# Splitting the first load into parts of every eighth partition, with one part loaded through GpSimd's queue

**Chip, cores, metric.** One core of one Trainium2 chip. Times are device microseconds (us) of one execution. A kernel's time is the median of its runs; the profile is of one of those runs, and its span is some 1.8 us shorter than the time.

## What the kernel computes

```python
x = abs(randn(32, 512, 1024)) + 1e-6          # float32, 67.1 MB
out = np.sum(1.0 / x, axis=-1)                # (32, 512) float32
```

The 16,384 rows of 1024 values lie as 128 partitions x 128 rows. For each of its rows a partition adds up the reciprocals; one half of a row is handled together with the other half, as (a + b) / (a * b), with the division done by logarithm and exponential.

Of the kernel before, what the change touches and what calls it, by code (L numbers as in the profile page):

```python
# [11 lines left out]
def kernel(  # L12
# [15 lines left out]
    nc = tc.nc  # L28
    f32 = mybir.dt.float32
    P = 128  # L30
    D = 1024
# [7 lines left out]


    A, B, C = (2, 0, 0), (2, 2, 0), (2, 2, 1)
    LOADS = [[A, B, A, B], [A, B, A, C]] * 5 + [[A, B], [A, C]] * 3



# [21 lines left out]
    x_v = x.flatten_outer_dims().rearrange("(p f) d -> p f d", p=P)  # L67
# [13 lines left out]
    opool = ctx.enter_context(tc.tile_pool(name="opool", bufs=1))  # L81
# [10 lines left out]
    ring = opool.tile([P, R, D], f32)  # L92
    sums = opool.tile([P, F], f32)
    ident = opool.tile([P, P], f32)
    make_identity(nc, ident)
    keep = tc.keep_in_program_order

    def add(bank, *halves):
        for k, half in enumerate(halves):
            i = nc.tensor.matmul(  # L100
                bank,
                lhsT=ident,
                rhs=half,
                start=k == 0,
                stop=k == len(halves) - 1,
            )
            keep(i)

    def sum_row(c, row, fac, out=None):
        i = nc.vector.tensor_tensor_reduce(  # L110
            out=row if out is None else out,
            in0=row,
            in1=fac,
            scale=S,
            scalar=0.0,
            op0=mult,
            op1=plus,
            accum_out=sums[:, c : c + 1],
        )
        keep(i)  # L120

    def sum_rows(c, xc, pr, sm, rc):
        m, e = xc.shape[1], len(sm)
        for j in range(e, m):
            row = xc[:, j, :].rearrange("p (h e) -> p h e", h=2)
            sum_row(
                c + j,
                row,
                rc[j - e].unsqueeze(1).to_broadcast([P, 2, H]),
                pr[:, e : e + 2, :] if j == e and e + 1 < m else None,  # L130
            )
        for j in reversed(range(e)):
            sum_row(c + j, pr[:, j, :], sm[j])

    waiting = None
    c0 = 0
    for chunks in LOADS:
        n = sum(m for m, _, _ in chunks)
        xt = ring[:, c0 % R : c0 % R + n, :]
        keep(nc.sync.dma_start(out=xt, in_=x_v[:, c0 : c0 + n, :]))  # L140

        made, q = [], 0
        for m, e, v in chunks:
            pr = ppool.tile([P, m, H], f32, tag="ps" if e else "pr")
            for j in range(v):
                b = bpool.tile([P, H], f32, tag="b")
                add(b, xt[:, q + j, H:])
                i = nc.vector.tensor_tensor(  # L148
                    out=pr[:, j, :], in0=xt[:, q + j, :H], in1=b, op=mult
                )  # L150
                keep(i)
            made.append(pr)
            q += m

        q = 0
        for (m, e, v), pr in zip(chunks, made):
            xc = xt[:, q : q + m, :]
            if v < m:
                i = nc.gpsimd.tensor_tensor(  # L159
                    out=pr[:, v:, :], in0=xc[:, v:, :H], in1=xc[:, v:, H:], op=mult  # L160
                )
                keep(i)
            sm = []
            for j in range(e):
                s = spool.tile([P, H], f32, tag="s")
                add(s, xc[:, j, :H], xc[:, j, H:])
                sm.append(s)
            if waiting:
                sum_rows(*waiting)
            keep(nc.scalar.activation(out=pr, in_=pr, func=Ln, scale=S))  # L170
            rc = []
            if e < m:
                r = rpool.tile([P, m - e, H], f32, tag="rc")
                keep(
                    nc.scalar.activation(out=r, in_=pr[:, e:, :], func=Exp, scale=-1.0)  # L175
                )
                rc = [r[:, l, :] for l in range(m - e)]
            if e:
                r = pr[:, :e, :]
                keep(nc.scalar.activation(out=r, in_=r, func=Exp, scale=-1.0))  # L180
            waiting = c0 + q, xc, pr, sm, rc
            q += m
        c0 += n
    assert c0 == LAST, c0

    c0 = LAST
    for n in LAST_LOADS:
        xt = ring[:, c0 % R : c0 % R + n, :]
# [17 lines left out]
    for op in order:  # L206
        kind, c, n = op[0], int(op[1:].rstrip("+")), 1 + op.endswith("+")
        j = (c - LAST) % 2
        rows = ring[:, c % R : c % R + n, :]
# [10 lines left out]
        elif kind == "V":  # L220
            keep(
                nc.vector.tensor_tensor(  # L222
                    out=pr[:, 0, :], in0=a[:, 0, :], in1=bs[c], op=mult
# [18 lines left out]
        elif kind == "T":  # L242
            row = rows[:, 0, :].rearrange("p (h e) -> p h e", h=2)
            k = (c - LAST) // 2
# [5 lines left out]
        elif kind == "X":  # L250
            keep(
                nc.scalar.activation(
                    out=rows,
                    in_=rows,
# [37 lines left out]
```

## The kernel before

The parts that matter here are the loads. `ring` holds 40 rows for each partition; a load brings 8 or 4 rows (later 2 or 1) of all 128 partitions, so a load of 8 rows is 128 packets of 32 KB, one for each partition. Sixteen DMA engines carry the packets, as the profile counts them; the trace before records sixteen partial landings for each of the 30 loads, on eight completion semaphores in turn, and a load has landed with the last of its sixteen (load 1: last one at 13.55 us, first multiply at 13.62).

```python
A, B, C = (2, 0, 0), (2, 2, 0), (2, 2, 1)     # a chunk: rows, rows with sums by TensorE, rows multiplied by VectorE
LOADS = [[A, B, A, B], [A, B, A, C]] * 5 + [[A, B], [A, C]] * 3
...
x_v = x.flatten_outer_dims().rearrange("(p f) d -> p f d", p=P)
ring = opool.tile([P, R, D], f32)
...
c0 = 0
for chunks in LOADS:
    n = sum(m for m, _, _ in chunks)
    xt = ring[:, c0 % R : c0 % R + n, :]
    keep(nc.sync.dma_start(out=xt, in_=x_v[:, c0 : c0 + n, :]))
    ...   # per chunk: GpSimd multiplies the halves (A), or TensorE adds them as well (B, C)
          # ScalarE: logarithm, then exponential; VectorE: product and row sum
```

## Time and profile before

| | before |
|---|---|
| time, median (lowest to highest) | 169.75 us (169.62 to 170.16), of three runs |
| read from HBM | 67.11 MB, 400 GB/s over the span of 167.9 us |
| busy share: TensorE, VectorE, ScalarE, GpSimd | 78%, 73%, 80%, 82% |
| DMA engines' share | 94.4% |

No compute engine is busy as much as the sixteen DMA engines are. The views that carry the argument are in the prediction. For the comparison below, here is the rate of the DMA engines in the profile's 40 slices (each 4.2 us), then three stretches from the table of stretches of the kernel before. The columns of a stretch: start and end, length, busy time and number of instructions of TensorE, its weight loads, VectorE, ScalarE and GpSimd, the granted clock of TensorE, the DMA share and GB/s. A packet is counted whole in the stretch where it starts, so that a share can come out above 1.

```profile
GB/s 195 429 437 429 445 429 437 437 429 429 406 455 414 445 422 449 422 431 437 429 429 429 429 398 429 427 433 433 420 429 408 423 418 424 422 422 414 382 26 18
```

### The profile page before, as it was taken

The numbers are of one execution on the slowest core, as the hardware profiler recorded it, in microseconds if no ns is written. First come the engines' busy times: TensorE is split into PE (matmuls) and PEld (weight loads), VectorE is DVE, ScalarE is ACT, GpSimd is POOL, SyncE is SP. The second block draws the span as 40 slices with busy tenths as digits, with TensorE's granted clock in tenths as the row PEclk, the third lists the DMA queues.
The fourth block names the chain that finished last, engine by engine and source line by source line (L and its number), as shares of the span: only waits on it lengthen the run. The fifth ranks groups of instructions, "written<-read, shape, count | busy, mean of one in ns | idle before, by whom it ended". The sixth has DMA issues, their size and how long they took to land.

```text
span 167.9 us, 1307 instructions
## 1 busy us (share of the span) xinstructions
PE 130.8 (78%) x278; PEld 50.5 (30%) x278; DVE 122.8 (73%) x268; ACT 134.1 (80%) x143; POOL 137.7 (82%) x73
## 2 busy tenths in 40 slices
PE   0007999786989869776797869877999988799991
PEld 0003333232323323222332323333343324243340
DVE  0000677768977677885777787778989898999894
ACT  3001898979888897959879787999999998999992
POOL 1007999699996999859996998999999999979780
PEclk9999999999999999999999999999999999999999
DMA  6999999999999999999999999999999999999900
GB/s 195 429 437 429 445 429 437 437 429 429 406 455 414 445 422 449 422 431 437 429 429 429 429 398 429 427 433 433 420 429 408 423 418 424 422 422 414 382 26 18
DMA packets 4471, 67.25 MB, mean 401 GB/s; under 512 B 496, under 2 KB 624, under 8 KB 1136
## 3 DMA queue, kind: packets, MB, share of 16 engines
q1 hardware_dynamic: 4464, 67.18, 94.4%
q8 instruction: 2, 0.03, 0.1%
q14 instruction: 5, 0.04, 0.1%
HBM read 67.11 MB, written 0.07 MB: 400 GB/s over the span
## 4 chain that ended last, share of the span: by engine, by line
DMA 71%; ACT 11%; POOL 10%; DVE 3%; issue 2%; PE 2%; DVEq 0%; SPq 0%; POOLq 0%; ACTq 0%
DMA ring<-in_x_dram 71%; POOL pr L159 8%; ACT pr L231 5%; ACT pr L237 3%; ACT r L237 2%; POOL pr L213 1%; DVE pr L110 1%; PE s L100 1%; DVE ring L110 1%; ACT pr L170 1%; ACT r L175 1%; PE bb L100 1%; DVE pr L222 0%; DVE sums L110 0%; DVEq L287 0%
## 5 line engine op out<-in xcount | busy, mean ns | idle before, releaser
L100 PE MATMUL s<-ring,ident 128*128 128x512 f32 x256 | 121.4, 613 | 32.2 <-DMA ring<-in_x_dram 16.2
L159 POOL TENSOR_TENSOR pr<-ring 128x1024 f32<-128x1024 f32 (+1 forms) x52 | 112.7, 2202 | 21.5 <-DMA ring<-in_x_dram 21.5
L100 PEld LDWEIGHTS s<-ring,ident 128*128 128x128 f32 x256 | 46.9, 193 | 104.1 <-issue 63.3
L170 ACT ACTIVATE pr<-pr 128x1024 f32<-128x1024 f32 x52 | 54.8, 1053 | 26.9 <-POOL pr L159 26.9
L110 DVE CUSTOM_DVE_ANT_1 pr<-ring,r 128x1024 f32<-128x1024 f32 x27 | 33.0, 1221 | 41.4 <-ACT r L175 41.4
L110 DVE CUSTOM_DVE_ANT_1 ring<-ring,r 128x1024 f32<-128x1024 f32 x37 | 44.8, 1217 | 0.2 <-issue 0.2
L110 DVE CUSTOM_DVE_ANT_0 pr<-pr,s 128x512 f32<-128x512 f32 x64 | 41.5, 683 | 0.3 <-ACT pr L237 0.3
L180 ACT ACTIVATE pr<-pr 128x1024 f32<-128x1024 f32 x26 | 27.5, 1057 | 0.8
L175 ACT ACTIVATE r<-pr 128x1024 f32<-128x1024 f32 x26 | 26.7, 1028 | 0.8
L213 POOL TENSOR_TENSOR pr<-ring 128x512 f32<-128x512 f32 (+1 forms) x15 | 24.5, 1648 | 3.0 <-DMA ring<-in_x_dram 2.4
L231 ACT ACTIVATE pr<-pr 128x512 f32<-128x512 f32 (+1 forms) x17 | 13.0, 794 | 1.0 <-DVE pr L222 0.7
L110 DVE DVE_READ_ACCUMULATOR2_ANT sums<- 128x1 f32 x128 | 10.6, 83 | 0.0
L100 PE MATMUL b<-ring,ident 128*128 128x512 f32 x16 | 8.7, 625 | 0.1
L237 ACT ACTIVATE pr<-pr 128x512 f32<-128x512 f32 (+1 forms) x10 | 6.9, 704 | 0.1
L237 ACT ACTIVATE r<-pr 128x512 f32<-128x512 f32 (+1 forms) x11 | 6.8, 625 | 0.1
L148 DVE TENSOR_TENSOR pr<-ring,b 128x512 f32<-128x512 f32 x8 | 5.5, 682 | 0.0
L100 PEld LDWEIGHTS b<-ring,ident 128*128 128x128 f32 x16 | 2.6, 188 | 5.6 <-DMA ring<-in_x_dram 4.1
L100 PE MATMUL bb<-ring,ident 128*128 128x512 f32 x6 | 3.2, 622 | 1.3 <-DMA ring<-in_x_dram 1.2
L222 DVE TENSOR_TENSOR pr<-ring,bb 128x512 f32<-128x512 f32 x3 | 2.1, 686 | 0.7 <-PE bb L100 0.6
L100 PEld LDWEIGHTS bb<-ring,ident 128*128 128x128 f32 x6 | 1.0, 188 | 3.4 <-DVE sums L110 2.0
L71 ACT ACT_TABLE_LOAD x1 | 1.3, 1283 | 0.7 <-PEq L276 0.7
L215 DVE TENSOR_TENSOR pr<-ring 128x512 f32<-128x512 f32 x1 | 0.9, 864 | 0.0
(6 smaller groups left out, 0.9 us busy)
## 6 DMA issues: line engine op xcount, KB each, us to landing
ring<-in_x_dram SPq DMA_DIRECT2D x10, 4096.0 KB, 37.8
ring<-in_x_dram SPq DMA_DIRECT2D x6, 2048.0 KB, 37.0
ring<-in_x_dram SPq DMA_DIRECT2D x10, 1024.0 KB, 26.0
ring<-in_x_dram SPq DMA_DIRECT2D x4, 512.0 KB, 16.8
out_dram<-sums SPq DMA_DIRECT2D x1, 64.0 KB, 1.5
```

The lines of the kernel that those rows point to most:

```text
L71: nc.scalar.add_instruction(mybir.InstLoadActFuncSet(name=nc.get_next_instruction_name(), act_func_set_id=act_sets.index("natural_log_exp_ ...
L100: i = nc.tensor.matmul(bank, lhsT=ident, rhs=half, start=k == 0, stop=k == len(halves) - 1,)
L110: i = nc.vector.tensor_tensor_reduce(out=row if out is None else out, in0=row, in1=fac, scale=S, scalar=0.0, op0=mult, op1=plus, accum_out ...
L148: i = nc.vector.tensor_tensor(out=pr[:, j, :], in0=xt[:, q + j, :H], in1=b, op=mult)
L159: i = nc.gpsimd.tensor_tensor(out=pr[:, v:, :], in0=xc[:, v:, :H], in1=xc[:, v:, H:], op=mult)
L170: keep(nc.scalar.activation(out=pr, in_=pr, func=Ln, scale=S))
L175: nc.scalar.activation(out=r, in_=pr[:, e:, :], func=Exp, scale=-1.0)
L180: keep(nc.scalar.activation(out=r, in_=r, func=Exp, scale=-1.0))
L213: keep(nc.gpsimd.tensor_tensor(out=pr, in0=a, in1=b, op=mult))
L222: nc.vector.tensor_tensor(out=pr[:, 0, :], in0=a[:, 0, :], in1=bs[c], op=mult)
L231: keep(nc.scalar.activation(out=pr, in_=pr, func=Ln, scale=S))
L237: keep(nc.scalar.activation(out=r, in_=pr, func=Exp, scale=-1.0))
```

## The change

The intent, as far as the code tells it: some DMA engines end later than others (in the kernel before the last load landed at 159.38 to 160.21 us on thirteen and at 161.29 to 161.46 on three), and moving one 16 KB packet from each of eight engines to the other eight should even this out. To do so, one half of the first load (rows 0 to 3) is cut into eight parts of 16 partitions each. Seven go by SyncE; the eighth goes by GpSimd's queue as two transfers of eight partitions, each behind a load of one element a partition into `spare` ("one-element load" below) that is meant to steer it onto one half of the engines. (The prediction calls the halves lower and upper; the traces do not number the engines.) The other half (rows 4 to 7) is loaded first and whole.

```diff
-    LOADS = [[A, B, A, B], [A, B, A, C]] * 5 + [[A, B], [A, C]] * 3
+    LOADS = [[B, B, A, A], [A, B, A, C]] + [[A, B, A, B], [A, B, A, C]] * 4
+    LOADS += [[A, B], [A, C]] * 3
...
+    spare = opool.tile([P, 1, 1], f32)
...
+    def first_load(xt, n):
+        h = n // 2
+        for g in range(0, P, P // 2):
+            for dst, rows, w in ((spare, 1, 1), (xt, h, D)):
+                at = slice(g, g + P // 2, 8)
+                keep(nc.gpsimd.dma_start(out=dst[at, :rows, :w], in_=x_v[at, :rows, :w]))
+        keep(nc.sync.dma_start(out=xt[:, h:, :], in_=x_v[:, h:n, :]))
+        for k in range(1, 8):
+            at = slice(k, P, 8)
+            keep(nc.sync.dma_start(out=xt[at, :h, :], in_=x_v[at, :h, :]))
...
-        keep(nc.sync.dma_start(out=xt, in_=x_v[:, c0 : c0 + n, :]))
+        if c0 == 0:
+            first_load(xt, n)
+        else:
+            keep(nc.sync.dma_start(out=xt, in_=x_v[:, c0 : c0 + n, :]))
```

More of the change, by code (lines that the diff above doesn't have):

```diff
@@ L133, in sum_rows @@
             sum_row(c + j, pr[:, j, :], sm[j])
+    def first_load(xt, n):
[3 more added lines that the diff above has]
+                at = slice(g, g + P // 2, 8)
+                keep(
+                    nc.gpsimd.dma_start(
+                        out=dst[at, :rows, :w], in_=x_v[at, :rows, :w]
+                    )
+                )
+        keep(nc.sync.dma_start(out=xt[:, h:, :], in_=x_v[:, h:n, :]))
+        for k in range(1, 8):
+            at = slice(k, P, 8)
+            keep(nc.sync.dma_start(out=xt[at, :h, :], in_=x_v[at, :h, :]))
     waiting = None
```

## The prediction

> **What bounds the kernel now.** I read the page first (slices, DMA rows, chain), then the table of stretches, the waits, the waits of the DMA-issuing queue, and the timeline of the first 14 us and of the tail.
>
> ```profile
> DMA  6999999999999999999999999999999999999900
> q1 hardware_dynamic: 4464, 67.18, 94.4%
> q8 instruction: 2, 0.03, 0.1%
> q14 instruction: 5, 0.04, 0.1%
> DMA 71%; ACT 11%; POOL 10%; DVE 3%; issue 2%; PE 2%; DVEq 0%; SPq 0%; POOLq 0%; ACTq 0%
> ```
>
> The DMA engines are full from slice 2 to slice 38, and the chain that ended last is 71% transfers. Two more queues, q8 and q14, carry seven small packets of instructions: whatever engine carries one of those loses time that the other fifteen do not lose.
>
> ```profile
> 1.70:13.60 11.90, 0.00 (x0) 0.00 (x0) 0.00 (x0) 0.32 (x1) 0.00 (x0) 1.00 1.02 413
> 60.00:100.00 40.00, 32.05 (x68) 12.01 (x68) 30.33 (x67) 33.60 (x33) 35.38 (x17) 1.00 1.00 427
> 155.00:161.50 6.50, 6.37 (x16) 2.65 (x15) 6.07 (x15) 6.44 (x11) 5.26 (x5) 1.00 0.71 284
> ```
>
> The last columns are the share and the rate of DMA. It runs at 413 GB/s before any engine computes, at 427 in the middle, and falls to a share of 0.71 in the last stretch: there some of the sixteen engines are through while others still load. That is what the change is after.
>
> ```profile
> 13.62 9.31 POOL L159 TENSOR_TENSOR pr<-ring 128x1024 f32<-128x1024 f32 x4 [12.32 <-DMA ring<-in_x_dram]
> POOL pr L159 <- DMA ring<-in_x_dram: 21.5, 10, 12.3
> SPq L140 <- DVE sums L110: 86.3, 11, 21.6
> 107.02 32.00 DMA ring<-in_x_dram
> 142.78 1.06 ACT pr L231
> ```
>
> GpSimd starts at 13.62, when load 1 has landed whole. Of its 21.5 us of waiting for loads, 12.3 are that start; the other 9.2 over nine loads are about 1 us of slack a load. In the chain (last two lines) transfers hold until 139.01; what follows is nearly all ScalarE, back to back from 142.78, whose own idle time before that is 0.67 us in the timeline. So a load stream that ends earlier helps by at most about 0.67 us; one that ends later shows in full.
>
> The trace also records the sixteen partial landings of every load. Load 1: 12.66 to 13.55, eight engines within 0.17 us and eight spread behind. The last load: 159.38 to 160.21 for thirteen engines, and 161.29, 161.31, 161.46 for three. Following them load by load, each step out of line coincides with one instruction packet: at 47.4 and 117.7 (+0.94, +0.96 on what looks like one engine of the early eight), at 66.1 and 134.9 (+1.54, +1.52 on two of the later eight), at 75.4 and 105.8 (+0.7 each, harmless). So three engines are some 1.2 us behind the fourth-last and set the end of the stream.
>
> [...]The trace has 32 KB packets of 1.21 us, 27.0 GB/s an engine[...].[...]
>
> **The change, part by part.** The order of instructions on PE, DVE and ACT differs only in that the first load's chunks come as B B A A instead of A B A B. Counts are the same, so no engine has more work.
>
> SyncE: one load becomes one half (rows 4 to 7, 2 MB) and seven parts of 16 partitions x 16 KB. An issue is 328 ns (median of SyncE's issues), so seven more are 2.3 us, while the half alone keeps the engines busy for 8 packets x 0.61 us (half of 1.21) = 4.9 us. Covered. Load 2 now waits for the half, because the eight completion semaphores are used up: it lands near 1.75 + 0.8 (the first packets take 2.0 instead of 1.2) + 4.9 = 7.4 us, when seven parts, 4.3 us, are still queued; issue to first packet took 1.0 us at the start. Covered too. Loads 3 to 5 wait for parts that land before 14 us, against a queue of ten us and more.
>
> GpSimd: four issues[...], inside its idle 12.3 us.
>
> Engines: each of the lower eight carries one 16 KB packet less in all (8 + 7 instead of 16), each of the upper eight one more (8 + 7 + 2). That is -0.6 and +0.6 us from then on. First compute comes when the upper half is done: 13.55 + 0.6 = 14.2 instead of 13.6; about 1 us of slack a load takes that up. At the end: if the three slow engines are of the lower half, they finish at 161.46 - 0.6 = 160.9, the unhindered upper ones at 160.2 + 0.6 = 160.8, balanced almost exactly, and the end comes 0.6 us earlier: 169.75 - 0.6 = 169.15. If they are of the upper half, it is 0.6 later: 170.35. I cannot name engines from this trace; two of the slow ones are of the late-starting eight, one of the early. The aim of the change suggests the lower half. I take 169.5 as the middle of this case, nearer to the first.
>
> **The rivals.**
> (1) [...]each of the seven parts takes 1.21 instead of 0.61 us: +4.3 us[...].[...] As the stream is full to the end, nothing takes this up: 169.75 + 4.3 to 5.3 = 174 to 175.[...] Against it: engines start up to 0.95 us apart (1.75 to 2.70), more than a packet, and a layout this elaborate on a kernel at 94% of its DMA was presumably tried for a gain. I give this 0.3.
> (2) The moved packets land on the wrong half[...]: 170.3 as above.
> (3) Instruction packets fall elsewhere: a changed instruction count on SyncE, GpSimd and PE (nine load semaphores to wait for instead of one) shifts the fetches. One at 1 us on another engine gives or takes up to 0.6 us.
> (4) The end is not set by the stream: ScalarE is continuous from 142.78. Then 169.7 whatever the balance.
>
> **Range and chances.** Cases (2) to (4) and the aim all lie in 168.9 to 170.4, about two thirds. Rival (1) at 174 to 175 takes 0.3. The range must reach into it: 168.8 to 174.6, with the point at 169.5. Faster by 2% would need 166.4, five times what the tail allows: 0.03. Slower by 2% is 173.1, which only rival (1) makes: 0.30. The rest, 0.67, within 2%.
>
> **What would show it.** Right: a first GpSimd multiply near 14.2; DMA share 1.0 in 1.7 to 13.6; the last landings closer together than 2.1 us, with the last near 160.9; ScalarE's idle before its piece at 142.8 gone. Wrong by rival (1): packets of the parts at 1.2 us instead of 0.6, a rate near 220 GB/s between 7 and 16 us, first multiply at 17 us or later, and every later landing some 4 us late. Wrong by (2): last landing near 162. By (4): landings earlier, end unmoved.

## More of the kernel before

```profile
3.00:7.00 4.00, 0.00 (x0) 0.00 (x0) 0.00 (x0) 0.00 (x0) 0.00 (x0) 1.00 0.89 385
8.00:14.00 6.00, 0.32 (x1) 0.35 (x2) 0.00 (x0) 0.00 (x0) 0.38 (x1) 1.00 1.01 437
14.00:20.00 6.00, 6.00 (x10) 2.46 (x10) 1.86 (x3) 3.75 (x4) 6.00 (x3) 1.00 1.00 431
```

About 430 GB/s (398 to 455) holds from the second slice to the last but four. The DMA share says how much of the time the engines had a packet in hand; the rate says how fast the packets went. Before the change the two move together.

## The result, and the profile after

The changed kernel takes **176.99 us** (176.73 to 177.60, five runs), the kernel before 169.76 us (169.62 to 170.16, five runs). The ratio is 1.043 (95%: 1.040 to 1.045): slower. A ratio is the mean time of one kernel's fast runs over the mean of the other's fast runs of the same rounds, so it is not quite the ratio of the medians.

First the DMA rows of the page after, and its chain by engine:

```profile
DMA  5999899998999999999999999999999999999800
GB/s 198 348 198 243 277 471 434 411 471 382 456 449 391 471 411 426 445 396 466 419 419 449 411 451 393 423 430 428 430 426 425 410 419 423 421 421 414 355 25 17
q1 hardware_dynamic: 4688, 66.91, 93.6%
q0 software_dynamic: 128, 0.26, 0.7%
...
DMA 54%; ACT 25%; POOL 8%; issue 6%; DVE 2%; PE 2%; SPq 1%; DVEq 0%; POOLq 0%; ACTq 0%
```

The DMA row still reads 8 or 9 in slices 2 to 38: a reader of that row alone sees nothing. The rate row beneath it falls to 198, 243 and 277 in slices 3 to 5 and is as before afterwards. The engines held packets all the time, but the packets were slow. The lower DMA share of the chain does not mean that transfers matter less: the chain changes over to ScalarE earlier, and ScalarE waits for loads that are late as a whole.

The same in the table of stretches after; the first three are those of the view before, the last one answers to the tail in the prediction:

```profile
3.00:7.00 4.00, 0.00 (x0) 0.00 (x0) 0.00 (x0) 0.00 (x0) 0.76 (x2) 1.00 1.02 430
8.00:14.00 6.00, 0.00 (x0) 0.00 (x0) 0.00 (x0) 0.00 (x0) 0.00 (x0) 1.00 0.95 188
14.00:20.00 6.00, 0.00 (x0) 0.00 (x0) 0.00 (x0) 0.00 (x0) 0.00 (x0) 1.00 1.07 259
...
60.00:100.00 40.00, 31.95 (x69) 11.98 (x68) 30.09 (x67) 33.38 (x32) 35.15 (x17) 1.00 1.00 429
160.00:169.00 9.00, 8.83 (x21) 3.70 (x20) 8.45 (x19) 8.61 (x14) 7.64 (x7) 1.00 0.69 277
```

Between 8 and 14 us the engines were busy at a share of 0.95 and moved 188 GB/s, where the kernel before had 1.01 and 437. The half load just before it ran at 430, and the middle of the kernel (60 to 100 us) runs at 429 again. So the loss lies in the time of the parts. GpSimd's four issues and its first multiply in the timeline after (start, length, engine, line, what, and in brackets the idle time before it):

```profile
1.44 0.72 POOL L147 DMA_DIRECT2D spare<-in_x_dram  x1
2.15 0.54 POOL L147 DMA_DIRECT2D ring<-in_x_dram  x1
2.69 0.53 POOL L147 DMA_DIRECT2D spare<-in_x_dram  x1
3.22 0.53 POOL L147 DMA_DIRECT2D ring<-in_x_dram  x1
...
20.70 9.29 POOL L183 TENSOR_TENSOR pr<-ring 128x1024 f32<-128x1024 f32 x4 [16.95 <-DMA ring<-in_x_dram]
```

The issues take 2.3 us in all, while GpSimd has nothing else to do. The first packet of its queue starts at 5.55 us, 4.1 after the first issue, and the first 16 KB packet at 6.79. The first multiply moved from 13.62 to 20.70 us. GpSimd's wait for loads in the table of waits after (total, times, longest):

```profile
POOL pr L183 <- DMA ring<-in_x_dram: 25.7, 10, 16.9
```

The longest one, at the start, grew from 12.3 to 16.9 us; without it the other nine waits together are 8.8 us, as before (9.2). The waits of the DMA-issuing queue after:

```profile
SPq L164 <- DVE sums L112: 76.6, 11, 17.1
SPq L164 <- DMA ring<-in_x_dram: 11.9, 7, 5.1
```

SyncE now waits 11.9 us for earlier loads, as the prediction said it would: load 2 lands on the semaphore of the half. The half landed whole at 11.16 us, where 7.4 was forecast, and SyncE issued load 2 at 11.18; experiments e1 and e8 below bear on whether such waits cost.

The trace records the sixteen partial landings of each load, and how long each packet took. These are readings of the record:

| | before | after |
|---|---|---|
| load 2, first eight landings | 22.37 to 22.55 | 28.16 to 28.77 |
| load 2, other eight | 22.69 to 23.23 | 29.66 to 30.18 |
| last load, first and last landing | 159.38, 161.46 | 165.23, 168.51 |
| 16 KB packet of the half load | (32 KB: 1.21) | 0.61 |
| SyncE's 16 KB packet of a part, 7 to 9 us | | median about 1.7, up to 1.84 and, rarely, 2.05 |
| 16 KB packet of a part, 9 to 17 us | | 1.12 to 1.26 for most |

The stream is 6.6 us late already at load 2 (the mean of the shifts of the two groups), stays so, and ends 7.05 us late; the kernel ends 7.23 us late. Among the last landings the spread grew from 2.08 to 3.28 us, where the change meant to reduce it. Following each engine through the record from packet to packet (a packet that starts where another ends is taken to be the same engine's), GpSimd's packets lie for the most part on the eight engines that start later (below: the later eight; those that start first are the early eight). Where engines end at nearly the same moment this following is not certain; but the packets of instructions on queue q8 agree with it: in the kernel before they delay engines of the later eight (by 1.54 us at 66.1 and 1.52 at 134.9), and the first of them, after the change (at 73.1), delays an engine of the eight that land later in the table (its next landing is at 79.99 us, 1.2 behind the next-latest). By the prediction's reading the later eight held two of the three latest engines.

### The profile page after: what moved, and what is told of

Same layout as the page of the kernel before. It is cut to its first block, busy times and chain, and to the rows that moved or that the text cites. A ratio compares the mean times of both kernels' runs of the same rounds, so it can differ in the third digit from the quotient of the medians.

```text
span 175.2 us, 1331 instructions
## 1 busy us (share of the span) xinstructions
PE 132.0 (75%) x278; PEld 52.1 (30%) x278; DVE 122.6 (70%) x268; ACT 134.3 (77%) x143; POOL 140.1 (80%) x77
## 4 chain that ended last, share of the span: by engine, by line
DMA 54%; ACT 25%; POOL 8%; issue 6%; DVE 2%; PE 2%; SPq 1%; DVEq 0%; POOLq 0%; ACTq 0%
DMA ring<-in_x_dram 54%; ACT pr L194 9%; POOL pr L183 7%; ACT pr L255 6%; ACT pr L204 4%; ACT pr L261 2%; ACT r L199 2%; ACT r L261 2%; POOL pr L237 1%; PE s L102 1%; DVE pr L112 1%; SPq L154 1%; DVE ring L112 1%; PE bb L102 0%; DVE pr L246 0%
## 5 line engine op out<-in xcount | busy, mean ns | idle before, releaser
L102 PE MATMUL s<-ring,ident 128*128 128x512 f32 x256 | 122.8, 623 | 37.9 <-DMA ring<-in_x_dram 22.0
L102 PEld LDWEIGHTS s<-ring,ident 128*128 128x128 f32 x256 | 48.4, 197 | 109.6 <-issue 72.5
L112 DVE CUSTOM_DVE_ANT_1 pr<-ring,r 128x1024 f32<-128x1024 f32 x27 | 33.0, 1220 | 16.9 <-ACT r L199 16.9
L147 POOL DMA_DIRECT2D spare<-in_x_dram x2 | 1.3, 626 | 0.1
```

The costliest lines, as they stand in the source:

```text
L102: i = nc.tensor.matmul(bank, lhsT=ident, rhs=half, start=k == 0, stop=k == len(halves) - 1,)
L112: i = nc.vector.tensor_tensor_reduce(out=row if out is None else out, in0=row, in1=fac, scale=S, scalar=0.0, op0=mult, op1=plus, accum_out ...
```

## Experiments

Theory P (partitions): 16 KB packets of a part take twice as long because of the set of partitions that the part writes. Why a set should be slow is not shown by any run here, and the sizes forecast under P are estimates. Rivals: the order of the rows, the many small transfers or their waits (O); the strided reading of HBM (S); GpSimd's own packets (G). Every run gave the reference's result except e3, whose wrong result is intended. A diff below is against the changed kernel unless it says otherwise; e1 to e5 and e8 all leave out GpSimd's four transfers, which is shown in e2's diff only.

| run | time, us (lowest to highest) | ratio to before (95%) |
|---|---|---|
| before | 169.76 (169.62 to 170.16) | |
| changed | 176.99 (176.73 to 177.60) | 1.043 (1.040 to 1.045) |
| e1, two whole-width halves | 169.60 (169.51 to 169.70) | 0.998 (0.996 to 1.000) |
| e2, eight parts by SyncE | 174.70 (174.64 to 174.74) | 1.028 (1.026 to 1.030) |
| e3, other source | 174.70 (174.51 to 174.83) | 1.028 (1.026 to 1.030) |
| e4, 16 neighbours a part | 181.90 (180.77 to 182.25) | 1.069 (1.064 to 1.074) |
| e5, every seventh | 173.88 (173.50 to 174.80) | 1.025 (1.021 to 1.028) |
| e6, before + 2 packets, partitions 64 up | 172.73 (172.48 to 174.93) | 1.020 (1.014 to 1.026), unclear |
| e7, before + 2 packets, partitions 0 up | 171.44 (171.29 to 173.64) | 1.013 (1.006 to 1.019) |
| e8, every fourth | 169.74 (169.71 to 169.84) | 0.999 (0.998 to 1.001) |
| e9, packets moved, every fourth | 172.78 (171.64 to 174.08) | 1.017 (1.010 to 1.025), unclear |
| e10, the same, other order | 172.81 (171.59 to 175.71) | 1.015 (1.008 to 1.022), unclear |
| e11, changed again | 177.60 (177.18 to 178.49) | 1.047 (1.043 to 1.051) |
| e12, before, first half earlier | 169.83 (169.76 to 169.93) | 1.000 (0.998 to 1.002) |

All these runs were fast but one of e10 (175.71, slow, not in its ratio). The medians of the kernel before in the first three sessions of experiments were 169.79, 169.84 and 169.87. Runs e13 to e16 are single looks, of unknown state.

### e1: the halves without the parts

```diff
-        # four GpSimd transfers; seven parts of every eighth partition
+        keep(nc.sync.dma_start(out=xt[:, :h, :], in_=x_v[:, :h, :]))
```

> The first load as two whole-width halves by SyncE, rows 4 to 7 ahead of rows 0 to 3, chunks in the order B B A A of the changed kernel; no parts, no GpSimd transfer. Theory[...]: none of its cause is here, so 169.8 us within 0.4, last landing of load 2 at 23.2, 16 KB packets of 0.61 us. Rival (order of chunks, the split itself, the later first compute or the waits for completion semaphores): 172 us or more.

Measured: 169.60 us, load 2 landed at 22.17 to 22.75, the 16 KB packets of the halves took 0.61 us. The stretch of e1:

```profile
8.00:14.00 6.00, 0.83 (x1) 0.50 (x2) 0.00 (x0) 0.00 (x0) 0.89 (x1) 1.00 1.10 472
```

Of O the order falls here: B B A A, the 16 KB packets and the split cost nothing. All 7 us come with the parts, GpSimd's included; whether their number and waits cost anything is left to e8.

### e2: all eight parts by SyncE

```diff
-        for g in range(0, P, P // 2):        # spare and part 0 by GpSimd
-            ...
-        for k in range(1, 8):
+        for k in range(8):
```

> As the changed kernel, but all eight parts of every eighth partition by SyncE and nothing by GpSimd. [...]eight packets an engine of 1.21 instead of 0.61 us, +4.5 to +4.9 us: 174.3 to 174.7 us, packets never 1.84. Rival (GpSimd's queue and its small packets slow the stream): 169.8 us. Rival (rows of memory 4 MB apart are slow to read)[...].

Measured: 174.70 us, +4.9 over before; packets of the parts 1.09 to 1.28 us from the second part on; load 2 at 27.40 to 28.04. The stretches of e2:

```profile
3.00:7.00 4.00, 0.00 (x0) 0.00 (x0) 0.00 (x0) 0.00 (x0) 0.00 (x0) 1.00 1.04 442
8.00:14.00 6.00, 0.00 (x0) 0.00 (x0) 0.00 (x0) 0.00 (x0) 0.00 (x0) 1.00 1.01 213
```

Beside a full share the rate is 213 GB/s, about half. Eight parts at 0.61 us extra each are 4.9 us: just the loss. So 4.9 of the change's 7.2 us need no GpSimd; the other 2.3 come with GpSimd's part. The 1.84 us packets never occur here, so they belong to that part too.

### e3: same destination, other source

```diff
-            at = slice(k, P, 8)
-            keep(nc.sync.dma_start(out=xt[at, :h, :], in_=x_v[at, :h, :]))
+            at, src = slice(k, P, 8), slice(16 * k, 16 * k + 16)
+            keep(nc.sync.dma_start(out=xt[at, :h, :], in_=x_v[src, :h, :]))   # wrong result on purpose
```

> As the eight parts by SyncE, but each part reads 16 neighbouring rows of the source (512 KB apart) into the same every-eighth partitions; the result is wrong on purpose. [...]the destination is the same, so the same time as the eight parts within 0.5 us, 174.3 to 174.7. Rival (the source's stride of 4 MB): back to 169.8 us.

Measured: 174.70 us, the same as e2 to the hundredth, 219 GB/s between 8 and 14 us. S falls: with rows 512 KB apart in the source in place of 4 MB the time is the same, as long as they go to the same partitions.

### e4: parts of neighbouring partitions

```diff
-        for k in range(1, 8):
-            at = slice(k, P, 8)
+        for k in range(8):
+            at = slice(16 * k, 16 * k + 16)
```

> Eight parts by SyncE of 16 neighbouring partitions each, right result. [...]each part takes 2.43 instead of 0.61 us, +13.5 to +14.6 us on the engines that come last: 183 to 184.5 us. Rival (source stride): 512 KB between rows is no worse than before, 169.8 to 174.5 us. Rival (a fixed cost of a part): as the eight parts.

Measured: 181.90 us (+12.1), packets 1.99 us. The stretches of e4:

```profile
8.00:14.00 6.00, 0.00 (x0) 0.00 (x0) 0.00 (x0) 0.00 (x0) 0.00 (x0) 1.00 1.00 128
14.00:20.00 6.00, 0.00 (x0) 0.00 (x0) 0.00 (x0) 0.00 (x0) 0.00 (x0) 1.00 1.01 131
```

The direction is P's: the same parts with other partitions in them take another time, 1.99 us a packet against 1.09 to 1.28 in e2. The size is not: I expected a quarter of the full rate (2.43 us a packet, 183 us or more), an estimate that no run bears out, and the trace has 128 to 131 GB/s. The time was a miss of 1 to 3 us. One thing can be read in the landings: the engines were further apart than a packet lasts (the landings of one part run from 19.33 to 21.89 us), so that two parts were under way at a time. So this run does not give the rate of one such part alone.

### e5: every seventh partition

```diff
-            at = slice(k, P, 8)
+            at = slice(k, 112, 7) if k < 7 else slice(112, P)
```

> Seven parts of every seventh partition (partitions k, k+7, ... of the first 112) and one of the last 16 partitions, all by SyncE; right result. [...]the seven parts lose little; the last part's 16 neighbours[...] cost up to 1.8 us: +2.3 us[...], 171.5 to 172.5 us, most packets of 0.61 us. Rival (fixed cost of a part, or the source's stride of 3.5 MB): as the eight parts of every eighth partition.

Measured: 173.88 us, load 2 at 27.01 to 28.50, 259 GB/s between 8 and 14 us. A miss: by P as I sized it the seven parts should have lost little, and the run lost 4.0 us. The packets of the seven parts took about 1.0 us (0.79 to 1.16), not 0.61, and those of the last part 1.3 to 2.0. Why the packets of every seventh partition lie between those of every fourth (0.61, e8) and of every eighth (1.09 to 1.28, e2), no run here shows.

### e8: every fourth partition, 32 at a time

```diff
-        for k in range(1, 8):
-            at = slice(k, P, 8)
+        for k in range(4):
+            at = slice(k, P, 4)
```

> Four parts of 32 partitions (every fourth) by SyncE, right result.[...] at one moment count: +4.1 to +4.9 us as with eight parts, 174 us.[...] by the whole transfer count: 169.8 us.

Measured: 169.74 us, no loss; packets 0.61 us. The stretch of e8:

```profile
8.00:14.00 6.00, 0.72 (x1) 0.50 (x2) 0.00 (x0) 0.00 (x0) 0.69 (x1) 1.00 1.12 478
```

I had expected 174, the first of the two outcomes; it is the second. So a strided part costs nothing in itself, nor do four transfers in place of one, with 5.9 us of SyncE's waits for earlier loads. Every fourth partition, 32 at a time, leaves a packet at 0.61 us, where every eighth, 16 at a time, makes it 1.09 to 1.28 (e2). How the partitions of a part were dealt to the engines, the runs do not show.

### e6, e7: what one extra packet costs, and into which partitions

Both add to the kernel before two transfers of eight 16 KB packets by GpSimd, behind `spare` loads, into rows of the ring that nobody reads before they are loaded again. The edit of e7; e6 has `(64, 65)`:

```diff
+    for g in (0, 1):
+        at = slice(g, g + 32, 4)
+        for dst, rows, w in ((spare, slice(0, 1), 1), (ring, slice(32, 36), D)):
+            n = rows.stop - rows.start
+            keep(nc.gpsimd.dma_start(out=dst[at, rows, :w], in_=x_v[at, :n, :w]))
```

> The kernel before, plus two extra GpSimd transfers of 8 partitions x 16 KB each, placed on one half of the engines by the two one-element loads as in the change, into slots that a later load overwrites. The partitions are 64, 68, ... 92 and their neighbours[...].[...] each upper engine gets two packets of 0.61 us more, the lower none: one group of eight landings of load 2 shifts by +1.2 us, the other by 0; about 171.0 us if the group that ends last is the upper one, 169.8 to 170.3 if it is the lower. Engines alone count: the same.

> As the extra transfers before, on the same engines, but into partitions 0, 4, ... 28 and their neighbours[...].[...] packets of both sides take 1.2 us while they overlap; the upper engines shift by +1.8 to +2.4 us and the lower ones, which carry nothing extra, by +1.2 us; about 172 us. Engines alone count: as the run before, upper +1.2, lower 0.[...]

The first stretch below is e6's, the second e7's:

```profile
8.00:14.00 6.00, 0.00 (x0) 0.00 (x0) 0.00 (x0) 0.00 (x0) 0.00 (x0) 1.00 1.06 377
```

```profile
8.00:14.00 6.00, 0.26 (x1) 0.29 (x2) 0.00 (x0) 0.00 (x0) 0.32 (x1) 1.00 1.01 434
```

In e7 no packet was stretched; the early eight engines took their two packets on top (landing of load 2 from 22.37 to 22.55 before to 23.49 to 23.76, +1.2, which is 2 x 0.61), the other eight stayed where they were, and three of four runs took 171.29 to 171.60, +1.6. The fourth, which is the profiled one, 173.64, lost the rest after its last load had landed at 162.48 (the store ended 8.4 us after that, in the kernel before 5.6); what happened there is said under e13 to e16. In e6 the same packets on the same eight engines were stretched to 0.61 to 1.14 us, and the 32 KB packets of SyncE beside them to as much as 1.92; load 2 landed at 24.14 to 25.21, and three of four runs took 172.48 to 172.78, +2.9. So into partitions 0 to 29 the extra packets of the early eight engines cost their own length: the mean landing of load 2 is 0.6 us later in e7, half of 2 x 0.61, since eight of sixteen engines carry them. Into partitions 64 to 93 the same packets delay SyncE's as well: the mean is 2.0 us later in e6. I had the two runs the wrong way round: the stretched packets were expected in e7. GpSimd's packets came on the early eight in both; why the partitions matter to them, the runs do not show.

### e9, e10: the intended balance without the parts of every eighth partition

SyncE loads parts of every fourth partition (free, by e8); GpSimd loads two rows of every fourth partition in four transfers of eight.

```diff
-        h = n // 2
-        for g in range(0, P, P // 2):
-            for dst, rows, w in ((spare, 1, 1), (xt, h, D)):
-                at = slice(g, g + P // 2, 8)
+        h, r = n // 2, n // 4
+        for g in range(0, P, 32):
+            for dst, lo, hi, w in ((spare, 0, 1, 1), (xt, r, h, D)):      # e10: xt first, then spare
+                at = slice(g, g + 32, 4)
...
-        for k in range(1, 8):
-            at = slice(k, P, 8)
+        for k in (1, 2, 3, 0):
+            at, e = slice(k, P, 4), h if k else r
```

> The change's shift of load between the two halves of the engines without its stride: SyncE takes rows 0 to 3 in parts of every fourth partition, which cost nothing (169.74 us), except for rows 2 and 3 of partitions 0, 4, ... 124; those 32 x 8 KB go by GpSimd in four transfers of 8 partitions, each behind a one-element load, all on one half of the engines. That half carries 16 KB an engine more than in the kernel before, the other half 16 KB less, as in the change. [...]the relieved half gains nothing and the loaded half loses about 1.2 us; if that is the half that starts later, it holds the two engines that come last, 171.0 us; if the other, 170 to 171 us. Engines alone count: +0.6 us or -0.6 us on the engines that come last, 169.2 or 170.4 us.

> As the run before, with each one-element load behind its real transfer instead of ahead of it, so that the real ones run on the other half of the engines. [...]no gain either, 170 to 171.2 us. Engines alone count: one of the two runs is at 169.2 us or close to it. In the trace the GpSimd packets of one run are on the eight engines that start first, of the other on the eight that start later.

Measured: neither gained. Of each, the two best runs took 171.6 to 171.8 us, some 1.9 more than before; the other two took 2 us or more on top of that. The last load landed at 162.3 in e9 and 162.6 in e10, against 161.5 before. In e9, whose profile is of a slower run (173.76 us), the store of the result ended 8.0 us after that, against 5.6 before, so that its further loss came after the stream. The spare loads did not steer: GpSimd's packets were on the early eight in both, so the comparison of the two halves that these runs were made for did not come about. What they do show is that 0.25 MB of packets taken from some engines and given to others bring nothing even without parts of every eighth partition. The landings say more than the time: load 2 landed at 23.37 and 23.43 us in the mean of the sixteen engines, in e8 at 22.51, although no bytes were added but the one-element loads. Had one half only gained what the other lost, the mean would have stayed. Two of the four transfers go to partitions 64 and up, where e6 had the early eight's packets stretched, to as much as 1.14 us.

### e11: the changed kernel again

> The changed kernel once more, on the chip and in the session of the two runs before. If the half that GpSimd's transfers land on is fixed by the program, its packets are again on the eight engines that start later, and 177.0 us. If it depends on what ran before (in the two runs with extra transfers they were on the eight that start first), they may be on the first eight now: then the last landings lie closer together and the time is 175.5 to 176.5 us.

Measured: 177.60 us; load 2 at 28.37 to 30.35, last landing 169.0, GpSimd's packets again on the later eight. The result repeats, also in which half was taken.

### e12: compute started earlier

```diff
 # in the kernel before
+        h = n // 2 if c0 == 0 else n
+        for at in (slice(0, h), slice(h, n))[: 1 + (h < n)]:
+            keep(nc.sync.dma_start(out=xt[:, at, :], in_=x_v[:, c0:c0 + n, :][:, at, :]))
```

> The kernel before with its first load as two whole-width halves, rows 0 to 3 first and chunks A B A B as they were, so that the engines start at 8 us instead of 13.6. Theory (the stream of loads is full to the end, so an earlier or later start of the engines is worth nothing): 169.4 to 169.9 us. Rival (the start of the compute engines is on the path): 165 us or less.

Measured: 169.83 us, no change, although the compute engines start 5 us earlier. The stretch of e12:

```profile
8.00:14.00 6.00, 5.50 (x10) 2.51 (x11) 1.04 (x1) 2.96 (x3) 5.35 (x3) 1.00 1.05 451
```

So a start of compute that comes earlier gains nothing here: what decides the end is when the stream ends. The late first multiply at 20.70 us of the changed kernel is a sign of the loss; by this run and by the landings, the loss itself is the 7 us of stream.

### e13 to e16: which half GpSimd's packets take

e13 is the changed kernel with `((xt, h, D), (spare, 1, 1))`, so the spare load behind; e14 is e7 with that order; e15 is e7 without spare loads; e16 is e7 with `slice(g, g + 64, 8)`.

> The changed kernel with each one-element load behind its real GpSimd transfer. If the one-element loads choose the half, the real packets are now on the eight engines that start first (in two profiles of the changed kernel they were on the eight that start later); if something else chooses it, they stay on the later eight. [...]174 to 178 us either way.

> The extra loads into partitions 0, 4, ... 28 (and neighbours) with the one-element loads last. If they choose the half, the packets move from the first eight engines to the later eight, [...]stretch from 0.61 to up to 1.2 us, 172.5 to 173.5 us. If not, no packet is stretched, 171.3 us.

> The extra loads without any one-element load. [...]the two real ones are on different halves: eight packets of 0.61 us and eight stretched ones. If not, all are alike. 170.5 to 172.5 us.

> The extra loads into every eighth partition, 0, 8, ... 56 and neighbours, one-element loads first[...]. If the stride of the partitions decides the half, the packets are on the later eight engines as in the changed kernel; if not, on the first eight as with stride 4[...]. 171 to 173 us.

| run | destination, order | GpSimd's packets on | packets | time, us |
|---|---|---|---|---|
| changed, e11 | every eighth, spare first | later eight | 0.61 to 1.84 (changed) | 176.99, 177.60 |
| e13 | every eighth, spare last | early eight | 0.61 to 2.13 | 177.13 |
| e16 | every eighth, spare first | later eight | 0.61 to 1.57 | 174.0 |
| e6, e7, e9 | every fourth, spare first | early eight | above | above |
| e10, e14 | every fourth, spare last | early eight | e14: 0.61 | 172.81, 174.0 |
| e15 | every fourth, no spare | early eight, both transfers | 0.61 | 171.39 |

In e13 the moved packets went to the other half, and the time is that of the changed kernel (177.13 and 176.99): which half gets them is not what costs. e16 beside e7 suggests why GpSimd's part is dear in the changed kernel: the same two packets per engine cost 4.3 us (one run) instead of some 1.6 once they go to every eighth partition and come on the later eight engines, with packets of up to 1.57 us instead of 0.61; which of the two does it, the run does not show. With every eighth partition the order of the spare loads decided the half (changed, e11 and e13); with every fourth it did not (e7 and e14), and I do not know why. e14 took 174.0, although its packets were not stretched: its last load landed at 162.84, much as in e7, and like e7's profiled run it lost the rest after that.

The traces show where these 2 us appear, and it is not in the loads. The tail has one multiply of VectorE that runs beside GpSimd's (the `D` of the order of the last rows). In the three profiles that lost the 2 us (e7, e9, e14) it starts about 0.1 us after a multiply of GpSimd has begun and takes 1.71 to 1.72 us; in the other fifteen profiles of this document it takes 0.85 to 0.88. In e7 it starts at 157.69 us and ends 2.4 us later than in e15, where it starts at 156.17; the run is 2.25 us longer. Why VectorE comes later there stays open.

No version tried beats the kernel before: e1, e8 and e12 equal it within 0.2%.

## Why the prediction was wrong, point by point

The prediction said 169.5 us, with 168.8 to 174.6 as the range; 176.99 lies outside. Its steps:

- **The bound.** Right. The stream is full to the end and nothing takes up a loss: the last landing came 7.05 us later, the end 7.23. e12 shows the converse, that an earlier start of compute gives nothing.
- **SyncE's issues and lane waits are covered.** Right in the result, though the seven issues took 4.92 us in all and not 2.3, the half landed whole at 11.16 us and not near 7.4, the parts that loads 3 to 5 waited for landed at 12.5 to 16.0 and not before 14, and the waits for earlier loads came to 11.9 us: e1 and e8, with such waits, lose nothing, and e2 with eight parts loses just what its packets explain.
- **GpSimd's four issues inside idle time.** Harmless as said; measured 2.3 us in all. The first packet came only 4.1 us after the first issue, where SyncE's first packet in the kernel before came 1.0 us after its issue; nothing shows that this cost anything by itself.
- **The failed step: "each of the lower eight carries one 16 KB packet less ... each of the upper eight one more", "-0.6 and +0.6 us from then on".** It counts packets and lets each of them last 0.61 us. In the parts of every eighth partition they last 1.2 us (e2: 1.09 to 1.28 us at 213 GB/s), in parts of every fourth 0.61 (e8), and with another source the time stays the same (e3: 174.70 us). That is the loss of 4.9 us of e2, against a balance term of 0.6.
- **Rival 1 was this loss, at 0.3.** Its size for the parts was right: 0.61 us a part, confirmed at 8 x 0.61 = 4.9 us in e2. What makes them last that long is not shown. What its range of 4.3 to 5.3 us left for GpSimd, 1 us by estimate, was too small: the changed kernel lost 2.3 us more than e2. About 1.5 us of that shows in the mean landing of load 2 (+6.6 us against +5.1 in e2), with packets at 1.84 us while GpSimd's were there; most of the rest is the wider spread between the two groups of engines. So even the rival's 174 to 175 was 2 us short.
- **Both arguments against rival 1 were poor.** That engines start up to 0.95 us apart did not help: in e2 they start from 1.74 to 2.54 us, further apart than a packet of 0.61, and the packets of the parts still took 1.09 to 1.28. That the layout "was presumably tried for a gain" is no evidence, and it lowered the chance of the case that came.
- **Case (2), the wrong half.** True as well: GpSimd's packets were on the later eight engines, which held two of the three latest, and the last landings spread over 3.28 us instead of 2.08. e13 puts them on the other half for the same time, so this decides little.
- **What would show it.** The signs named for rival 1 were the ones that came: packets of 1.2 us, 188 to 259 GB/s between 8 and 20 us (220 named), the first multiply at 20.70 (17 or later named), every later landing late (some 4 us named, 6 to 7 measured).

One thing that neither case asked: could the balance ever gain? e9 and e10 moved packets from some engines to others without parts of every eighth partition and found no gain: 171.6 to 171.8 us in the best runs, with load 2 landing at 23.37 and 23.43 us in the mean, against 22.51 in e8. They put the packets on one half only, so that the absence of a gain is supported and not shown.

## What to carry to other kernels

Judge the splitting of a load by the length of its packets in the partitions that each part writes, not by the number of DMA engines it occupies: parts of 16 partitions held the engines at a share of 1.00 to 1.01 and moved 213 GB/s (every eighth, e2) or 128 to 131 (neighbours, e4), while every fourth partition, 32 at a time, cost nothing here (e8). Where the transfers bound the kernel, read the rate row next to the busy row of the DMA engines: here a full share at half the rate was packets of 1.2 us in place of 0.61. Before a balance of half a microsecond is sought, price the packets that it adds by their length in the partitions they will go to, as e6 and e7 measure it, and give no weight to the thought that somebody must have tried it.
